# A projection block in another accumulator bank, weight splits among the squares, and warm-up work, in a two-layer decoder trunk

## The chip, the cores and the metric

The kernel runs on one core of one Trainium2 chip. The time is that of one execution on the device, in microseconds (us). The engines are TensorE (PE, its weight loads PEld), VectorE (DVE), ScalarE (ACT), GpSimd (POOL) and SyncE (SP), which only issues transfers. Each engine works through its own list of instructions in order.

## The reference

A trunk of two layers over 512 tokens of width 1024, in float32. Layer 0 mixes by two groups of attention heads behind one input projection, layer 1 by attention over selected keys; each is followed by a squared-ReLU MLP of width 4096.

```python
for layer in range(DEPTH):
    hn = rmsnorm(h, norm_mix[layer])
    if layer % 2 == 0:
        mix = even_mixer(hn, w_in_even[j], ...)   # differential and forgetting attention
    else:
        mix = odd_mixer(hn, w_in_odd[j], ...)     # indexer, top-k, attention on the kept keys
    h = h + mix
    h = h + sqrelu_mlp(rmsnorm(h, norm_mlp[layer]), w_mlp_in[layer], w_mlp_out[layer])
return rmsnorm(h, norm_final)

def even_mixer(h, w_in, ...):
    proj = h @ w_in                               # queries, keys, values of both groups, gates
    a_q, a_k = partial_rope(a_q), partial_rope(a_k)
    ...
```

## The kernel before

**Products.** Activations are held transposed, as eight tiles of 128 features by 512 tokens. Each matrix product is made with three matmuls for each tile of 128 by 128 weights: both factors are split into a high and a low part, and high x high, high x low and low x high are summed (gemm_steps, lines 348 to 355; L352, L353 and L354). A projection block of 128 output features is thus 8 x 3 = 24 matmuls of 128x512 into one bank. The high part is a cast on ScalarE (L157), the low part a subtraction on VectorE (L158), both in split.

**Weights.** emit_split takes the next 128 columns of weights in a fixed plan: it asks for the transfer (fetch, L284, tile raw, two buffers) and splits them into a tile whl (three buffers). A split can begin when the block three earlier has been multiplied.

**Start.** first_norm loads x, and norm writes for each of the eight tiles j the high part (L214, ScalarE) and the low part (L215, VectorE) of x times the norm's weight; the products of the first block follow them tile by tile (step). The tokens' norm factors are applied later, to the outputs. For them the eight tiles are squared (squares, L201 and L204 on ScalarE) and added (L205, VectorE), summed over features by eight small matmuls (L168), scaled (L171), raised to the power -0.5 on GpSimd (L173) and spread to all partitions (L180, L193, L194, L232). L235 multiplies the rotary tables csr by them. Six matmuls on ones into the bank pO (L130) run before, while the first data are on their way.

**Layer 0.** The projection blocks are named (i, a), with a = 0 query, 1 key, 2 value, in the plan's order (0,0), (0,1), (1,0), (1,1), (0,2), (2,0), ... Each goes to one of three banks "pg". A query or key is taken out of its bank by rope_from (L387 and L388 both read the bank, L389 and L390 finish) and split; halves of it are moved by transfers (L406). A value is scaled (L440) and transposed (L446). The loop over i in even weaves three or four threads: the scores of pair i (L477 to L485), the products of pair i-1, and gemm_thread(i) with the blocks (i+1,1), (i,2), (i+2,0). The differential attention's products use the one bank pO (L568 to L570). The table pick (L749) selects rows for a bias that is added to the scores from i = 4 on (L479 and L480).

**Order.** The order of instructions on each engine is set by a planner from priorities (the order in which the program names them) and modelled durations. `with tc.issue_after(ins)` puts every instruction of the block that runs on ins's engine behind ins on that engine; instructions of the block on other engines are not bound by it.

Of the kernel before, what the change touches and what calls it, by code (L numbers as in the profile page):

```python
# [10 lines left out]
F32 = mybir.dt.float32  # L11
# [3 lines left out]
OP = mybir.AluOpType  # L15
AX = mybir.AxisListType

P = 128
S = 512
D = 1024  # L20
NT = S // P
KB = D // P
# [27 lines left out]
V_FIRST = 2  # L50
DVE_ODD = 6
DVE_EVEN = 6
WARM = 6
PAD = 320
SHUF = list(range(8, 16)) + list(range(0, 8)) + list(range(16, 32))
OFF = [P * t * (t + 1) // 2 for t in range(NT + 1)]
# [22 lines left out]
def trunk(ctx, tc, packs, b_forget, lambda_q1, lambda_k1, lambda_q2, lambda_k2, rope, eye, xT, vecs, wpk, out):  # L79
    nc = tc.nc  # L80
# [47 lines left out]
    busy = pO()  # L128
    for i in range(WARM):
        nc.tensor.matmul(busy, onesf[:, :P], onesf, start=True, stop=True)  # L130
    nhalf = const.tile([P, NT], F32, name="nhalf")
    nc.gpsimd.memset(nhalf, -0.5)
    csr = const.tile([P, 2, S], F32, name="csr")
    r_b = const.tile([P, S], F32, name="r_b")

# [17 lines left out]
    hd = dram.tile([KB, P, S], F32, name="hd")  # L153


    def split(dst_hi, dst_lo, src, eng=None):
        nc.scalar.copy(dst_hi, src)  # L157
        (eng or nc.vector).tensor_sub(dst_lo, src, dst_hi.bitcast(F32))  # L158

    def small_loads():  # L160
        nc.gpsimd.dma_start(bf, b_forget.partition_broadcast(P).rearrange("p o d -> p (o d)"))
# [45 lines left out]
    def norm(gcol, rope_tab, step=None, lag=False):  # L207
        gh = []
        acc = scr()
        for j in range(KB):  # L210
            hi = blk("gh", 16, dt=F32R)
            lo = blk("gh", 16, dt=F32R)
            g = cols[:, gcol + j:gcol + j + 1]
            last = nc.scalar.activation(hi, h[j], AF.Copy, scale=g)  # L214
            nc.vector.scalar_tensor_tensor(lo, h[j], g, hi.bitcast(F32), op0=OP.mult, op1=OP.subtract)  # L215
            gh.append((hi, lo))
            if step:
                step(gh)
            if not lag:
                squares(acc, j)  # L220
        if lag:
            with tc.issue_after(last.ins):
                emit_split()
                for j in range(KB):
                    squares(acc, j)
        r_tables(rsqrt_cols(acc, 1.0 / D), rope_tab)
        return gh

# [8 lines left out]
    def first_norm(w, c0):  # L237

        fetch(2)
        for j in range(1, KB):  # L240
            load_x(j)
        pout = pg()
        gen = []

        def step(gh):
            j = len(gh)
            if j == 1:
                emit_split(2)
                wt = ready.pop(0)[0]
                gen.append(gemm_steps(pout, wt, gh))  # L250
                return
            next(gen[0])
            if j == KB:
                next(gen[0])
                nc.sync.dma_start(ident, eye)
                fetch()
                nc.sync.dma_start(csr, rope.rearrange("a p s -> p a s"))

        gh = norm(0, True, step, True)
        with tc.issue_after(root[0].ins):  # L260
            small_loads()
        with tc.issue_after(root[1].ins):
            emit_split()
        return gh, pout
# [104 lines left out]
            except StopIteration:  # L369
                live.remove(t)  # L370

    def block_steps(w, gh, c0, fin, put):

        wt = wnext(w, 0, c0)
        p = pg()
        for k, _ in enumerate(gemm_steps(p, wt, gh)):
            if k == V_LAG and vlate:
                vlate.pop(0)()
            yield
        fin(p, put)  # L380
        yield
# [355 lines left out]
    def even(ap, gh, p0):  # L737
# [8 lines left out]
        pick = ap.tile([P, 8, P], F32R, name="pick")  # L746
        rows = (pick, ck)
        nc.gpsimd.memset(ck.bitcast(F32), 0.0)
        nc.vector.tensor_tensor(pick, ident[:, 0:8, None].to_broadcast([P, 8, P]),  # L749
                                ident[:, 32:40, None].to_broadcast([P, 8, P]), op=OP.add)  # L750

        def gate_steps():
            fw = wnext(w, 0, 6 * S)
# [47 lines left out]
        def col(i, a):  # L801
            return (3 * (i // 4) + a) * S + (i % 4) * P

        def blk_steps(i, a):
            if i < 8:
                yield from block_steps(w, gh, col(i, a), (fq, fk, fv)[a][i // 4], (qs, ks, vs)[a].append)
                if (i, a) == GATE_AT:
                    yield from gate_steps()

# [9 lines left out]
        for i in range(9):  # L819
            th = []  # L820
            if i > 0:
                if raw_o:
                    th.append((subnorm_steps(*raw_o.pop(0)), 4))
                if i - 1 < 4:
                    th.append((diff_steps(ap, res, lambda o, j=i - 1: raw_o.append((*o, put_o(obs, j))), vs), 5))
                else:
                    th.append((pv_steps(ap, res, put_o(obs, i - 1), vs, dve=i > DVE_EVEN), 10))
                    hp = i - 5
            if i < 8:
                hp = i - 4  # L830
                if i < 4:
                    th.append((score_steps(ap, res, qs.pop(0), ks.pop(0), causal), 8))
                else:
                    th.append((score_steps(ap, res, qs.pop(0), ks.pop(0), causal, rows, (2 * hp, 2 * hp + 1)), 8))
                th.append((gemm_thread(i), 27 + (20 if i == GATE_AT[0] else 0)))
                if i == 0:
                    small_params()
            if EV_K[i]:
                th.append((early.steps(obs, EV_K[i]), 2 * (EV_K[i] - EV_K[i - 1])))
            weave(*th)  # L840
            while vlate:
                vlate.pop(0)()
# [193 lines left out]
```

## Time and profile before

| what | us |
|---|---|
| median of 3 runs | 1263.25 (1262.08 to 1263.38) |
| the profiled execution | 1262.1 |
| its span, first to last instruction | 1260.3 |
| TensorE busy | 1241.8 (99%) |
| VectorE busy | 720.6 (57%) |
| ScalarE busy | 559.9 (44%) |
| GpSimd busy | 96.9 (8%) |

Matmuls are pipelined and the profile models their ends, so a matmul's duration is longer than the distance to the next one. In the rows, a start and a duration come first; a bracket at the end gives the time that the engine had been idle before the instruction, and what released it. L352 is line 352 of the kernel. PEclk is the granted clock of TensorE: 1.00 is 2.4 GHz, 0.50 is 1.2 GHz.

### The profile page before, as it was taken

To read this page: it belongs to the slowest core of one execution; us is meant where nothing else is said; L and a number is where in the kernel's file an instruction comes from. 1 tells how busy PE (TensorE), PEld (TensorE's weight loads), DVE (VectorE), ACT (ScalarE), POOL (GpSimd) and SP (SyncE) were. 2 spreads that over 40 slices of the span, in tenths; PEclk is the share of its full clock that TensorE was granted. 3 is DMA by queue.
4 is the path that set the end of the run, shared out by engine and by line. 5 is a ranking of instruction groups with operands and counts; after the bars stand their busy time and mean duration, and the time that the engine had idled before them with its cause. 6 is when DMAs were issued, how large, how long until landed. Compare 5 with 4: busy or idle time off the path is not lost.

```text
span 1260.3 us, 15430 instructions
## 1 busy us (share of the span) xinstructions
PE 1241.8 (99%) x5854; PEld 1027.3 (82%) x5854; DVE 720.6 (57%) x1359; ACT 559.9 (44%) x1014; POOL 96.9 (8%) x68
## 2 busy tenths in 40 slices
PE   7999999999999999999999999999999999999997
PEld 5878888888888888888788888877888888888887
DVE  7887669564432244434499987787644322444232
ACT  5456667443422134323353578885533222333231
POOL 1000000000000000000114533230000000000000
PEclk9999999999999999999999999999999999999999
DMA  6545342322232222233334344523222222222211
GB/s 208 138 112 156 98 141 83 111 100 100 101 101 100 86 86 95 101 117 110 134 101 156 101 119 116 153 76 134 100 101 95 82 93 99 100 100 100 101 67 67
DMA packets 36298, 136.82 MB, mean 109 GB/s; under 512 B 5440, under 2 KB 5568, under 8 KB 26240
## 3 DMA queue, kind: packets, MB, share of 16 engines
q1 hardware_dynamic: 35504, 134.63, 32.8%
q0 software_dynamic: 304, 0.66, 0.3%
q8 instruction: 46, 0.75, 0.2%
q10 hardware_dynamic: 416, 0.55, 0.1%
q14 instruction: 28, 0.23, 0.1%
HBM read 111.18 MB, written 4.19 MB: 92 GB/s over the span
## 4 chain that ended last, share of the span: by engine, by line
PE 91%; DVE 3%; ACT 2%; issue 1%; DMA 1%; SPq 0%; POOL 0%; POOLq 0%; DVEq 0%; ACTq 0%
PE pg L352 27%; PE pg L354 27%; PE pg L353 27%; PE pT L511 2%; PE pS L477 1%; PE pS L478 1%; PE pO L530 1%; PE pO L529 1%; PE pT L168 1%; DVE whl L158 1%; ACT P L485 1%; PE pT L446 1%; ACT whl L157 0%; DVE P L483 0%; DVE PT L158 0%
## 5 line engine op out<-in xcount | busy, mean ns | idle before, releaser
L157 ACT CAST whl<-raw 128x1024 fp32r<-128x1024 f32 (+1 forms) x199 | 206.9, 1041 | 532.0 <-PE pg L354 489.0
L352 PE MATMUL pg<-gh,whl 128*128 128x512 f32 x1064 | 422.4, 398 | 6.2 <-DVE scr L388 3.6
L354 PE MATMUL pg<-gh,whl 128*128 128x512 f32 x1064 | 417.0, 392 | 0.4 <-DVE whl L158 0.3
L353 PE MATMUL pg<-gh,whl 128*128 128x512 f32 x1064 | 416.8, 392 | 0.3 <-DVE gh L215 0.3
L158 DVE TENSOR_TENSOR whl<-raw,whl 128x1024 fp32r<-128x1024 f32 (+2 forms) x175 | 211.6, 1209 | 179.0 <-ACT whl L157 178.7
L352 PEld LDWEIGHTS pg<-gh,whl 128*128 128x128 f32 x1064 | 200.1, 188 | 46.0 <-DVE scr L388 4.1
L354 PEld LDWEIGHTS pg<-gh,whl 128*128 128x128 f32 x1064 | 200.2, 188 | 42.9 <-DVE whl L158 1.1
L353 PEld LDWEIGHTS pg<-gh,whl 128*128 128x128 f32 x1064 | 200.5, 188 | 39.2 <-DVE gh L215 0.8
L352 PE MATMUL pg<-act,whl 128*128 128x512 f32 (+1 forms) x528 | 202.1, 383 | 0.0
L354 PE MATMUL pg<-act,whl 128*128 128x512 f32 (+1 forms) x528 | 202.0, 383 | 0.0
L353 PE MATMUL pg<-act,whl 128*128 128x512 f32 (+1 forms) x528 | 202.0, 383 | 0.0
L686 DVE SCALAR_TENSOR_TENSOR t<-pg,r_b 128x512 f32<-128x512 f32 x64 | 44.3, 692 | 156.1 <-PE pg L354 153.5
L352 PEld LDWEIGHTS pg<-act,whl 128*128 128x128 f32 x528 | 99.2, 188 | 19.5
L354 PEld LDWEIGHTS pg<-act,whl 128*128 128x128 f32 x528 | 99.2, 188 | 19.3
L353 PEld LDWEIGHTS pg<-act,whl 128*128 128x128 f32 x528 | 99.2, 188 | 19.2
L485 ACT ACTIVATE P<-P,sm 128x128 f32<-128x128 f32 (+3 forms) x128 | 71.7, 561 | 48.5 <-DVE sm L483 48.2
L639 DVE TENSOR_TENSOR h<-h,pg 128x512 f32<-128x512 f32 x46 | 31.3, 686 | 106.6 <-PE pg L354 106.6
L158 POOL TENSOR_TENSOR whl<-raw,whl 128x1024 fp32r<-128x1024 f32 x24 | 57.7, 2404 | 122.3 <-ACT whl L157 100.8
L173 POOL TENSOR_TENSOR sm<-sm,nhalf 128x4 f32<-128x4 f32 (+1 forms) x10 | 12.3, 1226 | 651.0 <-DVE sm L171 651.0
L158 DVE TENSOR_TENSOR PT<-pT,PT 128x384 fp32r<-128x384 f32 (+1 forms) x84 | 49.8, 597 | 19.0 <-ACT PT L157 18.4
L157 ACT CAST PT<-pT 128x384 fp32r<-128x384 f32 (+1 forms) x84 | 42.4, 510 | 14.2 <-PE pT L511 13.3
L511 PE MATMUL pT<-ident,P 128*128 128x128 f32 x280 | 46.6, 276 | 1.7 <-ACT P L498 0.9
(198 smaller groups left out, 1160.9 us busy)
## 6 DMA issues: line engine op xcount, KB each, us to landing
raw<-in_wpk_dram SPq DMA_DIRECT2D x78, 1024.0 KB, 4.8
raw<-in_wpk_dram SPq DMA_DIRECT2D x39, 512.0 KB, 3.9
qk<-qk SPq DMA_DIRECT2D x156, 128.0 KB, 2.3
hx<-in_xT_dram SPq DMA_DIRECT2D x8, 256.0 KB, 4.8
h<-in_xT_dram SPq DMA_DIRECT2D x8, 256.0 KB, 5.1
hd<-h SPq DMA_DIRECT2D x8, 256.0 KB, 2.0
h<-hd SPq DMA_DIRECT2D x8, 256.0 KB, 4.7
out_dram<-y SPq DMA_DIRECT2D x4, 512.0 KB, 3.0
```

Of the source, the lines that this page charges most:

```text
L157: nc.scalar.copy(dst_hi, src)
L158: (eng or nc.vector).tensor_sub(dst_lo, src, dst_hi.bitcast(F32))
L168: nc.tensor.matmul(p[:, t:t + 1], sq[:, t * P:(t + 1) * P], ones1, start=True, stop=True)
L352: nc.tensor.matmul(pout, wt[:, 0, k, :n], a, start=start and k == 0, stop=False)
L353: nc.tensor.matmul(pout, wt[:, 0, k, :n], b, start=False, stop=False)
L354: last_mm[0] = nc.tensor.matmul(pout, wt[:, 1, k, :n], a, start=False, stop=stop and k == KB - 1)
L446: nc.tensor.transpose(q[:, t * P:(t + 1) * P], y[:, t * P:(t + 1) * P], ident)
L477: nc.tensor.matmul(sp[m][:, c], qb[m][:, q], kb[0][m][:, :w], start=True, stop=False)
L485: nc.scalar.activation(o, o, AF.Exp, bias=st[m][:, t:t + 1], scale=-1.0, accum_out=st[m][:, 4 + t:5 + t])
L511: nc.tensor.transpose(p[:, o - o0 + (t - kt) * P:o - o0 + (t - kt + 1) * P], pt[:, OFF[t] + kt * P:OFF[t] + (kt + 1) * P], ident)
L639: nc.vector.tensor_add(h[j], h[j], p)
L686: nc.vector.scalar_tensor_tensor(t, p, 0.0, r_b, op0=OP.max, op1=OP.mult)
```

## The change

WARM goes from 6 to 8 dummy matmuls, and REST adds up to four dummy matmuls into the same bank behind the first groups of the first block (entry j - 1 is used at step j; step 1 returns before it gets there). A power on a tile of ones is computed on GpSimd at the start. split remembers its two instructions in parts_of, and norm uses that to place the squares: all behind the second split's cast, a third split's subtraction behind the addition of square 5, square 6 behind that split's cast. The split that first_norm places behind the last addition is then the fourth. Block (1,1) is multiplied into pO instead of a bank pg. The table pick is computed in the loop pass i = 3, behind the last split's subtraction, instead of at the head of even.

```diff
-WARM = 6
+WARM = 8
+REST = (0, 2, 1, 1)
...
+    ones4 = lpool.tile([P, NT], F32, name="ones4")
+    nc.gpsimd.memset(ones4, 1.0)
+    warm4 = lpool.tile([P, NT], F32, name="warm4")
     nhalf = const.tile([P, NT], F32, name="nhalf")
     nc.gpsimd.memset(nhalf, -0.5)
+    nc.gpsimd.tensor_tensor(warm4, ones4, nhalf, op=OP.pow)
...
+    parts_of = []
+
     def split(dst_hi, dst_lo, src, eng=None):
-        nc.scalar.copy(dst_hi, src)
-        (eng or nc.vector).tensor_sub(dst_lo, src, dst_hi.bitcast(F32))
+        parts_of[:] = [nc.scalar.copy(dst_hi, src),
+                       (eng or nc.vector).tensor_sub(dst_lo, src, dst_hi.bitcast(F32))]
...
         if lag:
             with tc.issue_after(last.ins):
                 emit_split()
-                for j in range(KB):
+            with tc.issue_after(parts_of[0].ins):
+                for j in range(KB - 2):
                     squares(acc, j)
+            with tc.issue_after(root[1].ins):
+                emit_split()
+            with tc.issue_after(parts_of[0].ins):
+                squares(acc, KB - 2)
+            squares(acc, KB - 1)
...
             next(gen[0])
+            if j <= len(REST):
+                with tc.issue_after(last_mm[0].ins):
+                    for i in range(REST[j - 1]):
+                        nc.tensor.matmul(busy, onesf[:, :P], onesf, start=True, stop=True)
...
-    def block_steps(w, gh, c0, fin, put):
+    def block_steps(w, gh, c0, fin, put, bank=None):
 
         wt = wnext(w, 0, c0)
-        p = pg()
+        p = (bank or pg)()
...
-        nc.vector.tensor_tensor(pick, ident[:, 0:8, None].to_broadcast([P, 8, P]),
-                                ident[:, 32:40, None].to_broadcast([P, 8, P]), op=OP.add)
+
+        def pick_rows():
+            nc.vector.tensor_tensor(pick, ident[:, 0:8, None].to_broadcast([P, 8, P]),
+                                    ident[:, 32:40, None].to_broadcast([P, 8, P]), op=OP.add)
...
-                yield from block_steps(w, gh, col(i, a), (fq, fk, fv)[a][i // 4], (qs, ks, vs)[a].append)
+                yield from block_steps(w, gh, col(i, a), (fq, fk, fv)[a][i // 4], (qs, ks, vs)[a].append,
+                                       pO if (i, a) == (1, 1) else None)
...
+                if i == 3:
+                    with tc.issue_after(parts_of[1].ins):
+                        pick_rows()
```

## Rows read from the trace of the kernel before

**Rows 1.** The chain that ended last, by engine, from the page.
```profile
PE 91%; DVE 3%; ACT 2%; issue 1%; DMA 1%; SPq 0%; POOL 0%; POOLq 0%; DVEq 0%; ACTq 0%
```

**Rows 2.** Stretches: length; busy (count) of PE, PEld, DVE, ACT, POOL; PEclk; DMA share, GB/s.
```profile
0.00:30.00 30.00, 24.19 (x88) 17.33 (x88) 22.48 (x36) 18.55 (x27) 6.28 (x15) 0.94 0.66 211
30.00:60.00 30.00, 28.30 (x124) 22.98 (x125) 26.56 (x71) 14.12 (x35) 0.00 (x0) 0.94 0.51 131
```

**Rows 3.** TensorE's waits from 40 us on: total us, times, longest.
```profile
PE pg L352 <- ACT whl L157: 1.3, 1, 1.3
...
PE pT L511 <- DVE P L496: 0.2, 1, 0.2
```

**Rows 4.** Timeline around the fourth block's start, VectorE and TensorE.
```profile
28.82 1.23 DVE L158 TENSOR_TENSOR whl<-raw,whl 128x1024 fp32r<-128x1024 f32 x1 [0.77 <-ACT whl L157]
...
30.57 0.68 DVE L388 TENSOR_TENSOR scr<-pg,csr 128x512 f32<-128x512 f32 x1
...
31.30 0.50 PE L352 MATMUL pg<-gh,whl 128*128 128x512 f32 x1 [3.64 <-DVE scr L388]
```

**Rows 5.** Half-microsecond stretches at the start, columns as in rows 2.
```profile
8.00:8.50 0.50, 0.50 (x2) 0.46 (x3) 0.50 (x1) 0.50 (x2) 0.00 (x0) 0.72 0.93 352
...
11.50:12.00 0.50, 0.50 (x3) 0.36 (x3) 0.50 (x1) 0.50 (x2) 0.19 (x1) 0.87 1.03 401
```

**Rows 6.** A stretch behind the wait: TensorE busy, clock, DMA share, GB/s.
```profile
32.00:32.50 0.50, 0.50 (x3) 0.61 1.00 410
```

**Rows 7.** Timeline of TensorE behind the wait.
```profile
32.12 0.62 PE L352 MATMUL pg<-gh,whl 128*128 128x512 f32 x1
...
35.52 0.40 PE L354 MATMUL pg<-gh,whl 128*128 128x512 f32 x1
...
36.92 0.39 PE L354 MATMUL pg<-gh,whl 128*128 128x512 f32 x1
```

**Rows 8.** Timeline of TensorE at the start.
```profile
1.52 2.93 PE L130 MATMUL pO<-onesf 128*128 128x512 f32 x6 [1.52 <-DVE onesf L125]
...
7.08 0.50 PE L352 MATMUL pg<-gh,whl 128*128 128x512 f32 x1 [0.69 <-ACT gh L214]
...
7.87 0.51 PE L353 MATMUL pg<-gh,whl 128*128 128x512 f32 x1 [0.28 <-DVE gh L215]
...
15.05 0.50 PE L354 MATMUL pg<-gh,whl 128*128 128x512 f32 x1 [0.30 <-DVE whl L158]
```

**Rows 9.** Timeline of the other engines at the start.
```profile
9.37 2.73 DVE L215 SCALAR_TENSOR_TENSOR gh<-hx,cols,gh 128x512 fp32r<-128x512 f32 x4
...
11.81 0.42 POOL L740 MEMSET mask<- 128x384 f32 x1 [10.69 <-DMA raw<-in_wpk_dram]
...
12.71 1.03 ACT L157 CAST whl<-raw 128x1024 fp32r<-128x1024 f32 x1
...
13.77 1.23 DVE L158 TENSOR_TENSOR whl<-raw,whl 128x1024 fp32r<-128x1024 f32 x1
...
17.10 1.22 DVE L749 TENSOR_TENSOR pick<-ident 128x1024 fp32r<-128x1024 f32 x1
...
18.24 1.48 DVE L205 TENSOR_TENSOR scr<-scr,scr 128x512 f32<-128x512 f32 x2
```

**Rows 10.** Timeline of VectorE and GpSimd around two powers.
```profile
20.95 1.23 DVE L158 TENSOR_TENSOR whl<-raw,whl 128x1024 fp32r<-128x1024 f32 x1
...
21.18 1.87 POOL L173 TENSOR_TENSOR sm<-sm,nhalf 128x4 f32<-128x4 f32 x1 [8.25 <-DVE sm L171]
...
106.00 1.22 DVE L158 TENSOR_TENSOR whl<-raw,whl 128x1024 fp32r<-128x1024 f32 x1
106.03 2.10 POOL L173 TENSOR_TENSOR sm<-sm,nhalf 128x4 f32<-128x4 f32 x1 [80.17 <-DVE sm L171]
```

**Rows 11.** Timeline of VectorE: its first wait for TensorE behind 32 us.
```profile
44.15 0.69 DVE L440 TENSOR_TENSOR scr<-pg,r_b 128x512 f32<-128x512 f32 x1 [0.43 <-PE pg L354]
```

**Rows 12.** Timeline of TensorE: the first attention product in pO.
```profile
85.37 0.48 PE L568 MATMUL pO<-PT,vs 128*128 128x512 f32 x1
```

## What the change should do to the time

> **What bounds the kernel now.** I read the chain that ended last first: 91% of it is TensorE [rows 1], so only a stretch in which TensorE stands, or runs at the lower clock, can be won back. Next came the stretches of 30 us. TensorE is busy 24.19 of the first 30 us and 28.30 of the next 30, with a mean granted clock of 0.94 in both [rows 2]. Behind 40 us there are seven waits of TensorE left, the longest 1.3 and the shortest 0.2, together 4.9 us over 1220 us [rows 3]. So what the change can win lies ahead of 40 us, and there I went through the timelines, engine by engine.
>
> The largest hole is one wait of 3.64 us: TensorE has ended the third projection block, (1,0), at 27.67 and starts the fourth, (1,1), at 31.30 [rows 4]. Its weights had long been split (the fourth split's subtraction on VectorE ended at 22.18 [rows 10]), and what released it was L388, the second of the two rotary products that read the first block's bank: three "pg" banks hold blocks 0 to 2 and the fourth block needs one of them back. VectorE came so late to L387 and L388 because the sixth weight split stood ahead of them in its queue. That split could be cast only when the third block had ended and freed its weight buffer, so VectorE waited 0.77 us for the cast and subtracted from 28.82 to 30.05 [rows 4]. Behind the hole the granted clock is halved, from 2.4 to 1.2 GHz: 0.61 in 32.0 to 32.5 [rows 6]. Eight matmuls start between 32.12 and 35.52, 0.425 us apart; the six behind them, to 36.92, 0.23 apart [rows 7].
>
> The clock falls once more at the start: 0.72 in 8.0 to 8.5, and up again within 11.5 to 12 (0.87) [rows 5]. Ahead of that fall TensorE had worked in pieces, with gaps of up to 0.69 us in which it waited for the normalised input [rows 8]. Late there, too, is the second weight split. Its raw weights had landed by 11.81, where a POOL instruction that waits for them goes on, but its cast ran at 12.71, behind three squares, and its subtraction at 13.77 to 15.0, and the third matmul of block (0,1) starts at 15.05 for that reason [rows 8, 9].
>
> **The change part by part.** *Bank.* Block (1,1) goes to pO, which only the warm-up used and which the attention products want first at 85.37 [rows 12]. Its rotary step would leave it by about 42, as VectorE's order stands now, so nobody waits for pO. The 3.64 us go. What is late next: (0,2) now asks for the first bank, 24 matmuls later. With the third block's end at about 26.8 (below) and 24 x 0.23 = 5.5 us for (1,1), that is at 32.3, where L388 ended at 31.25 in the trace of before. The cover is 1 us, and I price what may eat it under *Squares*. *Clock behind it.* Without the hole I take the second fall as gone: 8 x (0.425 - 0.23) = 1.56 us.
>
> *Second split ahead of the squares.* The cast can start at 11.81 instead of 12.71, so its subtraction at 12.87 instead of 13.77, and the matmul at 15.05 comes at 14.15: 0.90 us, if TensorE has ended block 0 by then. It ended it at about 14.1 (the matmul at 15.05 had waited 0.30, and the two ahead of it take 0.23 and a modelled 0.4), with some eight slow matmuls of the stretch from 8.3 to 11.7 in its way; at full clock it would end at about 12.6, half a us behind the last input part (VectorE, 12.1 [rows 9]). With the clock down as before the two first matmuls of (0,1) fill until 14.60 and the gain is 0.45. So this term is 0.45 to 0.90, and it depends on the dummy matmuls.
>
> *Dummy matmuls.* Two more at the start, at the pace of the six (2.93 us in all, so 0.43 to 0.49 each [rows 8]), end at 5.4 at the latest; only the first group can be late for them, and the second waits for its input until 7.08. Of REST, entries 2 to 4 act (at the first step the function returns earlier): two behind the first group, one behind each of the next two. They take 4 x 0.23 us in gaps such as 0.69 and 0.28 us where TensorE waits for the input [rows 8], so they cost nothing; if the cover is gone, 0.9. What they may do is hold the clock through 8.3 to 11.7. The trace shows the fall behind a stretch of broken work, no row shows it with the gaps filled; so the term keeps both ends. I take 0.90, since the full clock was there ahead of 8.3 with the six dummies and was lost only behind the broken stretch [rows 5]. The Trainium skill, "TensorE: Matmul & The Clock Gate", section "Why this matters for your kernels", advises only against long idle gaps between matmul bursts; by that alone the dummies between groups would be idle work, the start term 0.45 and the sum below 0.45 us smaller. The row speaks against it here: the clock fell behind gaps of 0.69 us at most [rows 5, 8].
>
> *Squares.* The third split now stands between square 5 and square 6, and all squares behind the second cast. VectorE, from 12.87: the subtraction 1.23, five additions of 0.74, the third subtraction 1.23, two additions: 12.87 + 2.46 + 7 x 0.74 = 20.5, where the additions of before ended at 19.72 [rows 9]. The table *pick* (1.22) is out of this stretch, and the third subtraction, which stood behind the additions, is in it: they balance. So the row factors come 0 to 0.9 us later than now, and with them L388: 31.25 to 32.1, still ahead of 32.3. If this misses, each us over 32.3 is a us of TensorE.
>
> *pick later.* 1.22 us of VectorE in the fourth loop pass, one pass ahead of its reader. VectorE has idle time even in the fullest stretch, 3.4 of 30 us [rows 2]: 0, at worst 1.22 if that place has none.
>
> *Dummy power.* The first power took 1.87 us, from 21.18, but VectorE's subtraction ran to 22.18 and the power ended 0.87 behind that; at 106.03 it took 2.10 and ended 0.91 behind a subtraction that began with it [rows 10]. So the long first one shows a wait for VectorE, not a first use: I take 0 and at best 0.87, and that off a chain which TensorE no longer waits for.
>
> *Given back.* This is the term that decides. TensorE comes 6.1 us earlier to everything behind (1,1), but VectorE doesn't: behind the hole it first waits for TensorE at 44.15 (0.43) [rows 11]. The rotary steps of four blocks and the splits are its work there, and their start hangs on the row factors, which don't come earlier. So TensorE runs up to 5 us ahead of VectorE around 43, covered by three banks of 5.5 us each. With 3.4 us of idle time in 30 to 60 VectorE recovers slowly; an evacuation (V's, or a score bank) that comes late then stands in TensorE's order. Ends: 0 (the banks cover it) and 4 (most of VectorE's lag). I take 1.0, nearest to the single waits there are behind 40 us [rows 3]. The planner lists the whole program anew by its own costs, so the seven later waits may move by about 1 us either way.
>
> **Sum.** 3.64 + 1.56 + 0.90 - 1.00 = 5.1 us off the profiled execution's 1262.1 (span 1260.3): 1257.0. The median of the runs, 1263.25, is 1.15 above the profiled one; from it the same gain gives 1258.1. I put 1257.5.
>
> **The rivals.** (a) Nothing is given back: 6.1 off, and the power's 0.87 where the splits lie better: 1255 to 1256. For it: three free banks and more than 40 us until pO is wanted. (b) VectorE becomes the bound until about 44, since its row factors come no earlier: TensorE wins the hole and stands again for the first scores or for V, with some 1.5 to 2.5 us left of the gain: 1260 to 1261.5. For it: VectorE waited for no matmul between the hole and 44.15; against it: TensorE has two blocks, (0,2) and (2,0), that need no new result of VectorE but a bank. The change not doing what it says ends here too: if L388 comes at 34 or later, (0,2) stands in the place of (1,1). (c) Slower than before: the hole moves to the first scores, whose key and query tiles need VectorE and then a transfer. If these come so late that TensorE stands about 6 us there and the clock falls behind it (1.56) as well as at the start, the loss is 6 + 1.6 + 1.2 (pick in a stretch without slack) - 6.1 = 2.7 us on the median: 1266. It decides from a wait of about 5 us; VectorE's 0.43 us of waiting at 44.15 speaks against a lag of that size.
>
> **How the numbers follow.** Forecast (1256.5 to 1259.5) 0.60, (a) 0.17, (b) 0.16, (c) 0.07. Range: 1254.5 takes in (a) with the power's 0.87, 1261 most of (b). A measurement of this kernel tells 0.2%, 2.5 us, from no change, so faster means under 1260.7: forecast, (a) and nearly half of (b), 0.83. Same: the rest of (b) and the mild part of (c), 0.12. Slower 0.05.
>
> **What would show it.** In the profile of the changed kernel: no wait of TensorE for L388, or a short one ahead of (0,2) instead of (1,1); a granted clock of 1.0 throughout 30 to 40; none of the half clock in 8 to 12, with dummies between the first groups (if it is there, the start term is 0.45); the second split's subtraction near 12.9; additions that end about 20.5; the row factors' power still near 1 or 1.9 us as a VectorE subtraction lies beside it; the end of (0,2), for which VectorE waited until 44.15, about 6 us earlier; and the waits behind 40 us, where the given-back part must stand. I'd be wrong in the first place if those waits grew from 4.9 to 8 us or more, or if the clock fell in 8 to 12 all the same and again later.

## The result, and the profile after

The changed kernel takes 1255.97 us (median of 4 runs, 1255.78 to 1256.62); the kernel before, run beside it, 1263.32 (4 runs, 1262.08 to 1264.38). The ratio is 0.9946, with a 95% interval of 0.9933 to 0.9958: faster by 0.5%. The profiled execution took 1255.86 us with a span of 1254.1, against 1262.1 and 1260.3 before, so 6.2 us less between two profiled executions.

The chain that ended last, by engine, answers to [rows 1]:

```profile
PE 90%; DVE 5%; ACT 2%; issue 1%; DMA 1%; POOL 0%; SPq 0%; DVEq 0%; POOLq 0%; ACTq 0%
```

It is TensorE as before, so the gain has to show as stretches in which TensorE stood or ran at the lower clock. The stretches, with the columns of [rows 2] (length; busy of PE, PEld, DVE, ACT, POOL; PEclk; DMA share, GB/s), answer to [rows 2, 5, 6]:

```profile
30.00:60.00 30.00, 29.89 (x144) 24.20 (x143) 29.80 (x78) 15.13 (x38) 0.00 (x0) 1.00 0.54 135
8.00:8.50 0.50, 0.50 (x4) 0.42 (x3) 0.50 (x2) 0.14 (x1) 0.00 (x0) 1.00 1.12 365
32.00:32.50 0.50, 0.50 (x4) 0.41 (x3) 0.50 (x2) 0.00 (x0) 0.00 (x0) 1.00 0.25 98
```

Both falls of the clock are gone: 1.00 where [rows 5] had 0.72 and [rows 6] 0.61. The pace says the same: four matmuls stand in each of the two half microseconds, where two and three stood before. From 30 to 60 us TensorE is busy for 29.89 of 30 (28.30 before) with 144 matmuls instead of 124. VectorE is busy there for 29.80 of 30 (26.56 before): it is as full as TensorE, which matters below.

The timeline of TensorE (start, duration; in the bracket the idle time before and what released it) answers to [rows 4, 7, 8, 12]:

```profile
1.52 3.78 PE L131 MATMUL pO<-onesf 128*128 128x512 f32 x8 [1.52 <-DVE onesf L126]
...
8.21 0.39 PE L269 MATMUL pO<-onesf 128*128 128x512 f32 x1
...
14.54 0.51 PE L371 MATMUL pg<-gh,whl 128*128 128x512 f32 x1 [0.53 <-DVE whl L165]
...
26.55 0.39 PE L371 MATMUL pg<-gh,whl 128*128 128x512 f32 x1
26.77 0.39 PE L369 MATMUL pO<-gh,whl 128*128 128x512 f32 x1
...
32.46 0.39 PE L369 MATMUL pg<-gh,whl 128*128 128x512 f32 x1
...
77.20 0.39 PE L585 MATMUL pO<-PT,vs 128*128 128x512 f32 x1
```

Lines have moved: L369 to L371 are the three matmuls of a projection step (L352 to L354 before), L269 the dummies of REST, L405 the second rotary product (L388 before). Block (1,1) starts in pO at 26.77 without a wait, right behind the last matmul of the third block at 26.55; before it started at 31.30 [rows 4]. Block (0,2) starts at 32.46, again with no bracket; before it started at 38.51:

```profile
38.51 0.39 PE L352 MATMUL pg<-gh,whl 128*128 128x512 f32 x1
```

Nobody waits for pO either: VectorE has read block (1,1) out of it by 40.72, and the first attention product wants it at 77.20.

The other engines, answering to [rows 9, 10, 11]:

```profile
1.24 1.02 POOL L137 TENSOR_TENSOR warm<-ones,nhalf 128x4 f32<-128x4 f32 x1
...
12.18 1.05 ACT L164 CAST whl<-raw 128x1024 fp32r<-128x1024 f32 x1 [0.78 <-DMA raw<-in_wpk_dram]
...
13.26 1.23 DVE L165 TENSOR_TENSOR whl<-raw,whl 128x1024 fp32r<-128x1024 f32 x1 [1.05 <-ACT whl L164]
...
19.42 1.48 DVE L212 TENSOR_TENSOR scr<-scr,scr 128x512 f32<-128x512 f32 x2
...
20.82 1.22 DVE L165 TENSOR_TENSOR whl<-raw,whl 128x1024 fp32r<-128x1024 f32 x1
...
22.29 1.01 POOL L180 TENSOR_TENSOR sm<-sm,nhalf 128x4 f32<-128x4 f32 x1 [7.19 <-DVE sm L178]
...
27.02 1.05 ACT L164 CAST whl<-raw 128x1024 fp32r<-128x1024 f32 x1 [2.21 <-PE pg L371]
...
28.10 1.23 DVE L165 TENSOR_TENSOR whl<-raw,whl 128x1024 fp32r<-128x1024 f32 x1 [2.14 <-ACT whl L164]
29.24 1.29 DVE L248 TENSOR_TENSOR csr<-csr,r_b 128x512 f32<-128x512 f32 x2
...
31.17 0.68 DVE L405 TENSOR_TENSOR scr<-pg,csr 128x512 f32<-128x512 f32 x1
...
41.93 0.69 DVE L457 TENSOR_TENSOR scr<-pg,r_b 128x512 f32<-128x512 f32 x1
```

The second split's cast now starts when its raw weights land, at 12.18. The additions of squares end at 20.90 (19.42 + 1.48). The sixth split still stands ahead of the readers of the first bank in VectorE's queue, and VectorE now waits 2.14 us for its cast at 28.10 (0.77 before [rows 4]); L405 ends at 31.85, 0.6 us ahead of (0,2), which wants that bank. One more thing has changed places: L248, which multiplies the rotary tables by the spread row factors, now stands behind the sixth split, while before (L235 there) it ran ahead of it:

```profile
26.77 1.28 DVE L235 TENSOR_TENSOR csr<-csr,r_b 128x512 f32<-128x512 f32 x2
```

TensorE's waits from 40 us on (total, times, longest) answer to [rows 3], all of them:

```profile
PE pg L369 <- ACT whl L164: 1.3, 1, 1.3
PE pT L900 <- DVE scr L897: 1.1, 1, 1.1
PE pT L528 <- ACT P L515: 0.8, 2, 0.6
PE pT L806 <- DVE sm L803: 0.6, 1, 0.6
PE pT L528 <- DVE PT L165: 0.6, 1, 0.6
PE pT L528 <- DVE P L513: 0.3, 1, 0.3
```

Again seven waits, together 4.7 us (4.9 before). What is won ahead of 40 us is kept: block (0,2) starts 6.05 us earlier (32.46 for 38.51) and the span ends 6.2 earlier.

### The profile page after: what moved, and what is told of

Its sections match the earlier page's. It is cut to its first block, busy times and chain, and to the rows that moved or that the text cites. A ratio compares the mean times of both kernels' runs of the same rounds, so it can differ in the third digit from the quotient of the medians.

```text
span 1254.1 us, 15436 instructions
## 1 busy us (share of the span) xinstructions
PE 1240.1 (99%) x5860; PEld 1026.7 (82%) x5860; DVE 719.6 (57%) x1359; ACT 559.4 (45%) x1014; POOL 97.3 (8%) x70
## 4 chain that ended last, share of the span: by engine, by line
PE 90%; DVE 5%; ACT 2%; issue 1%; DMA 1%; POOL 0%; SPq 0%; DVEq 0%; POOLq 0%; ACTq 0%
PE pg L369 27%; PE pg L371 27%; PE pg L370 27%; PE pT L528 2%; PE pS L495 1%; PE pS L494 1%; PE pO L547 1%; PE pO L546 1%; PE pT L175 1%; DVE P L500 1%; ACT P L502 1%; ACT whl L164 1%; PE pT L463 1%; DMA raw<-in_wpk_dram 0%; DVE whl L165 0%
## 5 line engine op out<-in xcount | busy, mean ns | idle before, releaser
L369 PE MATMUL pg<-gh,whl 128*128 128x512 f32 (+1 forms) x1056 | 418.0, 397 | 1.5 <-ACT whl L164 1.5
L371 PE MATMUL pg<-gh,whl 128*128 128x512 f32 (+1 forms) x1056 | 412.9, 392 | 0.6 <-DVE whl L165 0.5
L370 PE MATMUL pg<-gh,whl 128*128 128x512 f32 (+1 forms) x1056 | 412.7, 391 | 0.3 <-DVE gh L222 0.3
L371 PEld LDWEIGHTS pg<-gh,whl 128*128 128x128 f32 (+1 forms) x1056 | 197.9, 187 | 42.5 <-DVE whl L165 1.7
L369 PEld LDWEIGHTS pg<-gh,whl 128*128 128x128 f32 (+1 forms) x1056 | 198.0, 188 | 40.6 <-ACT whl L164 2.9
L370 PEld LDWEIGHTS pg<-gh,whl 128*128 128x128 f32 (+1 forms) x1056 | 198.3, 188 | 39.4 <-DVE gh L222 0.8
L369 PE MATMUL pg<-act,whl 128*128 128x512 f32 (+1 forms) x528 | 202.1, 383 | 0.0
L371 PE MATMUL pg<-act,whl 128*128 128x512 f32 (+1 forms) x528 | 202.0, 383 | 0.0
L369 PEld LDWEIGHTS pg<-act,whl 128*128 128x128 f32 x528 | 99.2, 188 | 19.3
L371 PEld LDWEIGHTS pg<-act,whl 128*128 128x128 f32 x528 | 99.2, 188 | 19.2
```

Source lines behind the costliest of these rows:

```text
L369: nc.tensor.matmul(pout, wt[:, 0, k, :n], a, start=start and k == 0, stop=False)
L370: nc.tensor.matmul(pout, wt[:, 0, k, :n], b, start=False, stop=False)
L371: last_mm[0] = nc.tensor.matmul(pout, wt[:, 1, k, :n], a, start=False, stop=stop and k == KB - 1)
```

## The experiments

The theory after the result: the time comes from three places ahead of 40 us, the bank wait (3.6), the clock behind it (1.5 to 2) and the start (some 0.7 to 1), and nothing is lost behind them. The rivals are that another part of the change carries the gain (start, dummies, order of VectorE), and that only VectorE's later order keeps the readers of the first bank in time.

**The bank alone** (e1_bank_only): the kernel before with the fourth block in pO, nothing else.

```diff
-        p = pg()
+        p = (bank or pg)()
...
+                                       pO if (i, a) == (1, 1) else None)
```

> Kernel of before with block (1,1) in pO and nothing else. My sum: the wait of 3.64 us and the eight slow matmuls behind it (1.56) go, so 5.2 us off, about 1258.1 on a median of 1263.3; the granted clock still falls at 8.3 and is whole from 12 on; TensorE goes from (1,0) to (1,1) at about 27.5 and finds the first bank free (its readers end at 31.25, asked for at 33.0). Rival, that the bank is worth less alone because VectorE takes over: over 1260, with a new wait of TensorE between 33 and 50. Rival, that the bank is all of the change: 1256.

Measured: 1257.31 us (1256.89 to 1258.67), ratio 0.996 (0.9946 to 0.9974), 5.4 less than the kernel before beside it; the span is 1255.1. The stretches of its trace at the start and behind the former wait:

```profile
8.50:11.50 3.00, 3.00 (x7) 2.39 (x8) 3.00 (x6) 3.00 (x6) 0.00 (x0) 0.50 1.03 356
...
32.00:32.50 0.50, 0.50 (x4) 0.42 (x3) 0.50 (x2) 0.00 (x0) 0.00 (x0) 1.00 0.63 246
```

The clock still falls at the start (0.50 from 8.5 to 11.5), as before the change, but no longer behind the third block. The bank's two terms, 3.64 + 1.56 = 5.2, are what it brings.

**All but the bank** (e2_all_but_bank): the changed kernel with the fourth block in pg.

```diff
-                                       pO if (i, a) == (1, 1) else None)
+                                       None)
```

> Changed kernel with block (1,1) back in a bank pg. My theory: what the other parts win at the start (0.7 us) only brings TensorE earlier to the same wait, which ends with the second reader of the first bank, and that came 0.6 later in the changed kernel (31.85 against 31.25). So a wait of about 5 us ahead of (1,1), the clock falls behind it, and the time is that of before or up to 0.6 above: 1263.3 to 1263.9. Rival, that each part is worth its own gain: 0.7 below before, 1262.6. Rival, that the row factors come earlier by the quicker power: below 1262.

Measured: 1263.56 us (1262.38 to 1264.5), ratio 1.0007 (0.9997 to 1.0016). Its wait, and a stretch behind it:

```profile
31.96 0.80 PE L369 MATMUL pg<-gh,whl 128*128 128x512 f32 x1 [4.73 <-DVE scr L405]
```

```profile
32.00:34.00 2.00, 2.00 (x5) 1.61 (x6) 2.00 (x4) 0.24 (x1) 0.00 (x0) 0.50 0.17 70
```

Everything else in the change is worth nothing without the bank: TensorE comes earlier to the third block's end and waits there 4.73 us instead of 3.64. What is won ahead of a wait goes into the wait. On top of the bank these parts do count: (0,2) starts at 32.46 in the changed kernel and at 33.12 in e1, and the spans are 1254.1 and 1255.1.

**The dummy matmuls** (e3_no_dummies): six at the start, none behind the groups.

```diff
-WARM = 8
-REST = (0, 2, 1, 1)
+WARM = 6
+REST = ()
```

> Changed kernel with the six dummy matmuls of before and none between the first groups. My theory: the clock falls from about 8.3 to 11.7 as before, block 0 ends at about 14.1 instead of 12.9, two matmuls of (0,1) follow to 14.6, and the split they then need is there at 14.5: 0 to 0.3 us lost, 1256.0 to 1256.3. Rival, that the dummies carry the part of the gain that the sum did not have (7.35 on the medians against 6.2 in the profiled executions): 1257 or more, and a larger spread of the runs.

Measured: 1256.09 us (1255.77 to 1256.53), ratio 0.9947 (0.9933 to 0.9962); the span is 1254.7, 0.6 above the changed kernel's. TensorE in it:

```profile
8.93 0.63 PE L371 MATMUL pg<-gh,whl 128*128 128x512 f32 x1
9.36 0.63 PE L369 MATMUL pg<-gh,whl 128*128 128x512 f32 x1
...
15.94 0.39 PE L371 MATMUL pg<-gh,whl 128*128 128x512 f32 x1
```

Without the dummies matmuls start 0.43 us apart until about 13.4, the pace of the lower clock in [rows 7], and the third matmul of (0,1) comes at 15.94 instead of 14.54. So the dummies do hold the clock, though not all of the 1.4 us is the clock's: in this execution the second group also got its input 0.7 us later (it starts at 7.55, for 6.85 in the changed kernel). Which of the dummies count, the two more ahead or the four within, was not tried. Of the 1.4 us, 0.8 are left where (1,1) starts (27.56 for 26.77) and 0.6 in the span; between the medians it is 0.1 (0.4 against the repeat below). Four or five runs can't tell any of these from nothing: the spans of e3's own runs go from 1254.0 to 1254.7.

**The old order of squares** (e4_old_squares): norm places the squares as before; all else as changed.

```diff
-                for j in range(KB - 2):
+                for j in range(KB):
                     squares(acc, j)
-            with tc.issue_after(root[1].ins):
-                emit_split()
-            with tc.issue_after(parts_of[0].ins):
-                squares(acc, KB - 2)
-            squares(acc, KB - 1)
```

> Changed kernel with the squares and splits in the order of before (one split ahead of them by priority only, the third behind the last addition). My theory: the second split's subtraction is back at 13.8, the third matmul of (0,1) at 15.05, and all behind it 0.5 later: 1256.5. The row factors come 0.3 to 0.6 earlier, which nobody uses. Rival: the row factors are what counts, no loss or a gain, 1256.0 or less.

Measured: 1258.66 us (1258.05 to 1259.2), ratio 0.9968 (0.9955 to 0.9981): 2.7 slower than the changed kernel, where half a us was expected. Its timeline tells why (L363 to L365 are the projection matmuls there, L399 the second reader of the first bank):

```profile
28.06 0.68 DVE L399 TENSOR_TENSOR scr<-pg,csr 128x512 f32<-128x512 f32 x1
...
41.26 0.50 PE L365 MATMUL pg<-gh,whl 128*128 128x512 f32 x1 [1.29 <-DVE whl L165]
```

The start loses 0.9 (the third matmul of (0,1) at 15.42). The rest is a side effect: in the new listing the sixth split's subtraction stands behind the rotary steps, at 39.99, and TensorE waits 1.29 us for it. The edges among the squares fix more of VectorE's order than the squares. So this run doesn't price the old order of squares by itself. It does show how early the readers can come: with the row factors spread by 26.08 and the sixth split behind it, L399 ends at 28.74, 3.1 us earlier than L405 in the changed kernel.

**pick early** (e5_pick_early): the table back at the head of even.

```diff
+        pick_rows()
...
-                if i == 3:
-                    with tc.issue_after(parts_of[1].ins):
-                        pick_rows()
```

> Changed kernel with the table pick computed at the head of the even stage again. If the planner puts it among the squares' additions, as in the kernel before, the row factors come 1.2 us later, the second reader of the first bank ends at 33.05 instead of 31.85, and TensorE, which asks for the bank at 32.46, waits 0.6 us ahead of (0,2): 1256.6. If it puts it into one of VectorE's gaps between 25.9 and 28.1, nothing changes: 1256.0.

Measured: 1255.99 us (1255.79 to 1256.52), ratio 0.995 (0.9934 to 0.9967). VectorE in it (L243 takes the row factors):

```profile
20.21 1.22 DVE L768 TENSOR_TENSOR pick<-ident 128x1024 fp32r<-128x1024 f32 x1
...
24.46 0.17 DVE L243 COPY rtm<-sm 128x4 f32<-128x4 f32 x1 [1.13 <-POOL sm L180]
...
28.28 1.29 DVE L248 TENSOR_TENSOR csr<-csr,r_b 128x512 f32<-128x512 f32 x2 [1.32 <-ACT r_b L245]
29.49 1.22 DVE L165 TENSOR_TENSOR whl<-raw,whl 128x1024 fp32r<-128x1024 f32 x1
...
31.23 0.68 DVE L405 TENSOR_TENSOR scr<-pg,csr 128x512 f32<-128x512 f32 x1
```

The row factors come 1.13 us later than in the changed kernel (24.46 for 23.33), but L405 only 0.06. So the table does stand among the additions (20.21), and the 1256.6 expected for that case is missed. In the changed kernel VectorE waited 2.14 us for the sixth split's cast; here it takes L248 first, waits 1.32 us for the spread row factors, and makes the split behind it. The table went into time in which VectorE had been idle.

**Later row factors** (e8_late_factors): pick computed three times at the head of even, to push the row factors past the bank's cover.

```diff
+        for _ in range(3):
+            pick_rows()
```

> Changed kernel with the table pick computed three times over at the head of the even stage: 3.7 us more of VectorE there. My theory, that the cover of the bank is 0.6 us and each us behind it is a us of TensorE: the bank is free at 35.5 instead of 31.85, a wait of about 3 us ahead of (0,2), and the clock may fall behind it (1.5 more): 1259 to 1260.5. Rival, that TensorE's lead is absorbed elsewhere and the wait is not paid at the end: 1256 to 1257.

Measured: 1256.44 us (1256.13 to 1257.51), ratio 0.9956 (0.9941 to 0.9971). VectorE (the fifth and sixth split, and the second reader) and the start of (0,2):

```profile
27.31 2.35 DVE L165 TENSOR_TENSOR whl<-raw,whl 128x1024 fp32r<-128x1024 f32 x2
...
31.51 0.68 DVE L405 TENSOR_TENSOR scr<-pg,csr 128x512 f32<-128x512 f32 x1
```

```profile
32.25 0.49 PE L369 MATMUL pg<-gh,whl 128*128 128x512 f32 x1
```

A miss: the row factors are 1.56 us later (L243 at 24.89), the readers only 0.34 (L405 ends at 32.19). The expectation took the row factors for what sets the readers, and left out that VectorE had idle time to fill: from 20 to 32 us it is busy for 8.55 of 12 us in the changed kernel and for 11.05 here, where the fifth and sixth split follow each other with no wait for a cast. That time is now used up: (0,2), at 32.25, finds its bank free by 0.06 us. What more work ahead of the split would cost was not tried.

**Later readers** (e11_late_readers): six extra products of 128x512 on VectorE between the sixth split and the products that the readers need.

```diff
+        if rope_tab and not delayed:
+            spare = scr()
+            for i in range(6):
+                delayed.append(nc.vector.tensor_mul(spare, r_b, r_b))
+            with tc.issue_after(delayed[-1].ins):
+                for i in range(2):
+                    nc.vector.tensor_mul(csr[:, i], csr[:, i], r_b)
```

> Changed kernel with six products of 128x512 on VectorE (0.6 us each) between the row factors and the rotary tables' products, so that the readers of the first bank come late for certain. In VectorE's order the seventh split then stands ahead of them, and its cast waits for the end of (1,1). My theory: the second reader ends about 36 instead of 31.85, TensorE waits about 3.7 us ahead of (0,2), and the clock may fall behind it: 1259.7 without the fall, 1261.3 with it. Rival, that the lead of TensorE is absorbed later and the wait not paid: below 1258.

Measured: 1262.94 us (1261.45 to 1264.03), ratio 1.0 (0.9991 to 1.0009); 7.2 more than the changed kernel run beside it, 6.3 in the span. VectorE's extra work and the second reader (L413 here), with a weight split at 34.98 between them; then (0,2):

```profile
29.54 4.32 DVE L250 TENSOR_TENSOR scr<-r_b 128x512 f32<-128x512 f32 x6
...
36.71 0.68 DVE L413 TENSOR_TENSOR scr<-pg,csr 128x512 f32<-128x512 f32 x1
```

```profile
37.45 0.79 PE L377 MATMUL pg<-gh,whl 128*128 128x512 f32 x1 [4.53 <-DVE scr L413]
```

```profile
38.00:40.00 2.00, 2.00 (x6) 1.57 (x5) 2.00 (x6) 0.62 (x1) 0.00 (x0) 0.50 0.00 0
```

The readers end at 37.39 instead of 31.85: 5.5 us later, of which 0.6 is cover, 0.3 a later start of TensorE in this execution ((1,1) at 27.07 for 26.77) and 4.53 a wait, with the lower clock behind it. The wait is longer than expected (3.7), and the time 1.6 above the 1261.3. This gives back the whole gain: readers that come late are paid in full and with the clock on top.

**The wait filled** (e7_filled_hole): the kernel before with 14 matmuls of no use behind the third block, so that TensorE works where it waited.

```diff
+        with tc.issue_after(last_mm[0].ins):
+            for i in range(14):
+                nc.tensor.matmul(busy, onesr, gh[0][0], start=True, stop=True)
```

> Kernel of before, with the bank as it was, and 14 dummy matmuls of 128x512 into the unused bank pO behind the last matmul of (1,0), where TensorE waits 3.64 us. They take 14 x 0.23 = 3.2 us of the wait and leave the wait's end where it is. My theory that the clock's fall is a price of its own behind the wait: the eight matmuls from 32.1 on run at full clock, 1.5 us won, 1261.2 on a median of 1262.7. Rival, that the clock falls for another reason, or that the dummies hold up the row factors' sums: no gain or a loss, 1262.7 or more.

Measured: 1260.19 us (1259.65 to 1261.5), ratio 0.9985 (0.9976 to 0.9994); the span is 1258.5. TensorE:

```profile
27.89 3.43 PE L820 MATMUL pO<-gh,onesr 128*128 128x512 f32 x14
31.69 0.50 PE L352 MATMUL pg<-gh,whl 128*128 128x512 f32 x1 [0.38 <-DVE scr L388]
...
37.27 0.39 PE L352 MATMUL pg<-gh,whl 128*128 128x512 f32 x1
```

Block (1,1) starts 0.4 later than before (31.69), but its matmuls follow at the pace of the full clock (in the trace 0.23 apart from 32.03 on): to the start of (0,2) at 37.27 it takes 5.58 us, for 7.21 before. So the clock behind the wait costs 1.6 us in that block (the sum had 1.56). At the end the gain is 1.8 in the span and 2.1 between medians, more than the 1.2 by which (0,2) starts earlier; one of the waits of before behind 40 us, 0.4 for a score bank at 46.76, is gone as well. So the two terms of the bank can be told apart: of e1's 5.4 the clock is 1.6 to 2.1 and the wait itself the other 3.3 to 3.8.

**The changed kernel again** (e0_changed_again), beside the next two and e11.

> The changed kernel itself, beside the next three on the same chip: 1256.0, with the spread of its runs below 1 us.

Measured: 1255.73 us (1255.41 to 1259.26, 5 runs), ratio 0.9949 (0.9937 to 0.9962). The median is as expected, the spread is not: one of the five took 1259.26. No trace of that execution was kept, so its cause is open.

**The second split in halves** (e9_halves): its raw weights come in two transfers and it is cast and subtracted in two halves.

```diff
-                emit_split()
+                emit_split(2)
...
-                fetch()
+                fetch(2)
```

> Changed kernel with the second weight split, and its load, in two halves as the first has them. The casts and subtractions of 0.6 us each then let TensorE begin (0,1) with the first half: its third matmul at about 13.5 instead of 14.54. My theory that the cover of the first bank moves with TensorE, since its readers stand behind the sixth split, which the third block's end releases (4.9 us to the second reader's end against 5.5 us of block (1,1)): everything 0.9 earlier, 1255.1. Rival, that the row factors bind now: a wait of 0.3 to 0.9 ahead of (0,2), 1255.5 to 1256.0.

Measured: 1255.05 us (1254.48 to 1255.53), ratio 0.9937 (0.9925 to 0.995): 0.7 less than the changed kernel beside it, and below both kernels. The second split's cast starts at 11.56. The start of (1,1) and the sixth split's cast:

```profile
25.30 0.39 PE L369 MATMUL pO<-gh,whl 128*128 128x512 f32 x1
...
25.81 1.05 ACT L164 CAST whl<-raw 128x1024 fp32r<-128x1024 f32 x1 [1.54 <-DMA raw<-in_wpk_dram]
```

The time is the one expected, but by two errors that cancel: block (1,1) starts 1.5 us earlier than in the changed kernel, not 0.9, and only about half of that arrives at the end. There is no wait ahead of (0,2), since the readers come 1.2 us earlier too. The cover shrinks to 0.4: the sixth split's cast now waits for its raw weights, 0.6 us past the third block's end. Of the lead, 0.7 is left at the first attention product in pO (76.50 for 77.20); a wait of 0.4 us for a score bank, at 64.59, lies ahead of it. The changed kernel has no such wait.

**A second bank lent** (e10_halves_two_banks): on top of that, block (0,2) into one of the banks of the scores.

```diff
-                                       pO if (i, a) == (1, 1) else None)
+                                       {(1, 1): pO, (0, 2): pS}.get((i, a)))
```

> The same with block (0,2) in a score bank, which nobody wants before 44. If the row factors bind in the kernel with halves alone, this takes the wait away: 1255.1, and below that kernel by the wait. If they don't: the same as that kernel, or up to 0.5 worse where the first scores then find one bank less.

Measured: 1260.63 us (1259.94 to 1263.42), ratio 0.9981 (0.9972 to 0.999). The trace is of the slowest of the eleven executions (1263.42). The start of the second group, the matmul that waits for a weight split, and the stretch behind:

```profile
8.10 0.50 PE L369 MATMUL pg<-gh,whl 128*128 128x512 f32 x1 [1.17 <-ACT gh L221]
...
43.90 0.79 PE L371 MATMUL pg<-gh,whl 128*128 128x512 f32 x1 [2.99 <-DVE whl L165]
```

```profile
44.00:46.00 2.00, 2.00 (x7) 1.71 (x8) 2.00 (x3) 0.62 (x1) 0.00 (x0) 0.50 0.55 129
```

Banks are no longer what TensorE waits for: the planner listed the blocks in another order ((0,2) itself starts only at 50.04), a weight split came late in VectorE's full queue (42.64), and the wait of 2.99 us and the lower clock stand there. So the run doesn't answer what was asked of it; it shows a hole that moves, after a new listing. It also has a fall of the clock at the start in spite of the dummies: TensorE waits 1.17 us for the input of the second group, and from 9.23 to 12.22 matmuls start 0.43 us apart.

## Why the prediction was right, and where its sum was off

The forecast was 1257.5 (1254.5 to 1261.0), faster: the measured 1255.97 lies within that range, but below the forecast's own 1256.5 to 1259.5 and where rival (a), nothing given back, had put it (1255 to 1256). Point by point:

**Bank and clock behind it: right.** The sum had 5.2; e1 alone gave 5.4, with no wait for L388. Where TensorE stood shows the same: (1,1) starts 4.53 us earlier and (0,2) 6.05, so 1.52 for the clock, or 1.75 if one counts that a matmul which spreads the row factors (0.23) ran inside the third block before (L194) and runs inside (1,1) now (L201). e7 gives that term a direct price of 1.6 in the block and 1.8 to 2.1 at the end.

**Second split ahead of the squares: right in kind, a term mis-sized.** The sum took 0.90 because it let the cast start at 11.81, where a GpSimd instruction that waits for the same raw weights had gone on [rows 9]. In the changed kernel the cast waits 0.78 us for the landing until 12.18, the subtraction runs at 13.26 instead of 12.87, and the third matmul of (0,1) is 0.51 earlier (14.54 for 15.05). By the third block's end the lead is 0.73 (the last matmul starts at 26.55, before at 27.28), but 0.23 of it is the matmul that moved out of this block, so the term is worth 0.5. The limit was the landing, which the sum took from one execution; with the same load it let the cast start at 11.88 in e8 and at 12.62 in e3. The low end of the term, 0.45, is near what came, but it was meant for a clock that falls, and the clock did not fall. With the transfer and the split in halves (e9) the cast starts at 11.56 and 0.7 us more is won.

**Dummy matmuls: right in kind.** They hold the clock from 8 to 12 in the changed kernel, and no wait shows a cost. In the four traces without them (the kernel before, e1, e3, e7) matmuls start 0.43 us apart from 9.5 to 11; in eight of the nine with them 0.23 or little more. The ninth is e10's, with the wait of 1.17 us ahead. What they bring at the end, 0.1 to 0.4 between medians and 0.6 between spans, can't be told from nothing; it doesn't contradict the 0.45 by which the sum let the start term depend on them.

**Squares and row factors: right outcome, wrong mechanism.** The additions ended at 20.90 (predicted 20.5), the second reader at 31.85 (predicted 31.25 to 32.1), and the cover ahead of (0,2) was 0.6 (predicted 1.0 at best, 0.2 at worst). But the step "the row factors come 0 to 0.9 us later than now, and with them L388" is not how it came about, so that the number fits is luck. The row factors come 0.25 us later (L243 at 23.33, for 23.08 before). Before, they were spread by 26.46 and the rotary tables done (L235) when the sixth split came, and the readers waited for that split alone. Now the spread ends at 28.55, because the planner lists it later on TensorE and, on ScalarE, behind the sixth split's cast; so VectorE makes the split, 0.72 earlier than before, and then L248 (1.29) ahead of the readers: 0.6 later in all. Row factors that come later still, by 1.13 in e5 and 1.56 in e8, move L405 by 0.06 and 0.34 only, since VectorE had idle time there. From the last matmul's modelled end, 26.94, to L405's end at 31.85 it is 4.9 us, against 5.5 for the 24 matmuls of (1,1): so the cover moves with TensorE, as far as the next limit allows (e9, 0.4 left). It is lost when work fills VectorE's idle time ahead of the split (e8, 0.06 left) or grows behind it (e11). "Each us over 32.3 is a us of TensorE" held in e11, with the clock behind it besides.

**pick later: 0.** e5 agrees (1255.99), within the half microsecond or so by which the medians of such runs differ.

**Dummy power: 0.** The first power on the chip, on the tile of ones at 1.24, takes 1.02 us, and the one at 22.29 takes 1.01, with VectorE's subtraction over by 22.04. In e1, which has no dummy, the first power is the long one again (1.87), beside a subtraction. In e4, which has the dummy, the second power is long all the same, beside a subtraction from 20.38 to 21.61:

```profile
20.54 1.93 POOL L180 TENSOR_TENSOR sm<-sm,nhalf 128x4 f32<-128x4 f32 x1 [7.23 <-DVE sm L178]
```

The power ended 0.86 behind it, and 0.88 in e1, as in [rows 10]. The Trainium skill, "SBUF — State Buffer", section "SBUF: two separate sides", has VectorE and GpSimd share a pair of ports under an exclusive lock, with the loser blocked for the whole instruction. The trace agrees: 1.01 to 1.02 us alone, and an end 0.86 to 0.91 behind that of the VectorE instruction beside it. The changed kernel's power is short because the new order lets the subtraction end first, not because of a dummy. A changed kernel without the dummy was not run.

**Given back: the term that failed.** The sum took 1.0 (0 to 4) off, and nothing was given back: the waits behind 40 us are 4.7 together (4.9 before), and the lead of 6.05 us at (0,2) is 6.2 at the first product of L546 (L529 before), much later (162.97 for 169.18), and 6.2 in the span. The lag of VectorE was read rightly: V's evacuation L457 runs at 41.93, 4 us behind TensorE's end of (0,2) at about 37.9, and VectorE is busy for 29.80 of 30 us. What was priced wrongly is what such a lag costs: with three banks of 5.5 us each between the two engines, 4 us is cover and not a wait. By this the term should have been 0 until the lag nears what the banks hold. That is rival (a), "three free banks and more than 40 us until pO is wanted". The reading comes from the trace; no run varies the lag alone. And the cover has an end: of another 1.5 us of lead, in e9, half is lost.

**Rivals (b) and (c) didn't come, but their mechanisms are real.** e11 shows (b), VectorE's readers as the bound, when they come 5.5 us later; e10 has a hole that moves, with the clock behind it, as (c) feared, but to a weight split in a new order of blocks and not to the first scores.

**The numbers.** 6.1 - 1.0 = 5.1 was predicted and 6.2 measured between the profiled executions: 1.0 of the difference is the given-back term. That the 6.1 ahead of it came out so well is in part luck. The lead of 6.05 at (0,2) is some 3.8 for the wait, 1.75 for the clock and 0.5 for the start, where the sum had 3.64, 1.56 and 0.90: errors of 0.4 that cancel. Half a us more is that 1257.5 was put above the 1257.0 that the profiled execution gives. Between medians the gain is 7.35 here, and 6.9 where the changed kernel ran again (1255.73 against 1262.64); the runs of the kernel before scatter by one to two us either way.

## What to carry to other kernels

A wait of the engine that sets the end costs its length and then the lower clock behind it, so a bank that is lent for one block can be worth half as much again as the wait that the profile shows. Before a gain ahead of a buffer wait is counted, see what sets the release: here a weight split, which waits for an earlier block, stood ahead of the readers in another engine's queue, so that work between that split and the readers counted in full, and work ahead of it was free as long as it fitted into the time in which that engine was idle. In these traces a lag of the second engine cost little as long as the banks between the two held it; compare the lag with the time that the banks hold before a part of the gain is taken off.

## What the runs showed of the hardware that was not expected

- The clock column can read 1.00 while matmuls run at the lower pace. In e3 the column gives 1.00 for 0 to 30 us, and the matmuls from 8.93 on start 0.43 us apart; in the changed kernel the eight dummies of the start take 3.78 us, the same pace. At the start of a trace the pace tells the clock, not the column.
- Gaps of quite different size stood ahead of the same lower clock: in the kernel before, broken work with gaps of up to 0.69 us [rows 5, 8], and in others waits of 4.73 (e2), 4.53 (e11) and 2.99 us (e10). In the changed kernel the broken work at the start, with two more dummies ahead of it and four within, kept the full pace; e10, with the same dummies and a gap of 1.17 us, lost it.
- The clock's share of a wait's price is large: 1.6 us in the block behind a wait of 3.64 (e7).
